# Another order of projection pairs, and two gate pairs moved into the attention, in a hybrid SSD and attention layer

## The chip, the cores and the metric

The kernel runs on one core of a Trainium2 chip. The metric is the device time of one execution in microseconds (us). The engines are TensorE (PE, its weight loads PEld), VectorE (DVE), ScalarE (ACT), GpSimd (POOL) and SyncE (SP), which issues most DMAs. Each engine works through its own instructions in order and waits on semaphores for the others.

## The reference

One layer over a sequence of 1024 positions with 1024 channels, all in float32, weights drawn at random. Cut to what matters:

```python
h = rmsnorm(x, pre_g)
z_ssm, xbc, dt_raw, q, k, v, f_raw, z_att, g_ssm, g_att = split(h @ w_in)
xbc = silu(causal_dwconv(xbc, conv_w, conv_b))         # 4 taps
xs, b, c = split(xbc)                                  # 16 heads of 64; 4 groups, state 128
y = ssd_chunked(xs, softplus(dt_raw + dt_bias), -exp(a_log), b, c, d_skip)   # chunks of 128
y_ssm = group_rmsnorm(y * silu(z_ssm)) * ssm_norm_g
log_f = log_sigmoid(f_raw + fgate_b)                   # per head
o = softmax(q k^T / 8 + F[t] - F[s], causal) @ v       # F = cumsum(log_f), 16 heads of 64
y_att = o * silu(z_att)
merged = sigmoid(g_ssm) * (y_ssm @ w_branch_ssm) + sigmoid(g_att) * (y_att @ w_branch_att)
out = x + rmsnorm(merged @ w_out, post_g)
```

## The kernel before

**Projections as a stream of pairs.** The large products (h times w_in, the two branch products and the last one) are cut into units of 128 output columns. Two units of one kind make a `Pair`, for instance ("z", 0) and ("z", 1). A pair is computed by a seven-product scheme of the Strassen kind over the two halves of the inner dimension, the two units and the two halves of the sequence. Each product is a step of 12 matmuls: four slices of the inner dimension, three matmuls each, since every operand is split into a rounded high part and a low rest (`h` and `l`; tiles `x0h`, `x0l` and so on for the moving side, `wop` for the weights). A step runs in two halves of 6 matmuls; a pair is 14 halves. Weights are prepared by sums (DVE, line 357 and others) and splits (ACT line 351, DVE line 352). Results are evicted by `keep` (ACT line 404) and `give` (lines 412 to 418), and a handler then does what the kind of pair needs: `conv` (b, c, x), `silu_gate` (z, za), `tanh_gate` (gs, ga), `parts` (q, k: high and low parts stored) or `values` (v: transposed on TensorE, later, by `turn_values()`). All but the convolution's results go to DRAM and come back when they are used.

**The order.** `order` lists the pairs of four groups, `late` the gates za (four), gs (three more) and ga (four), `ends` the branch products (wbs, wba) and the last product (merged). `Stream` runs them all in one sequence, and other work is put beside them by counting halves: `stream.halves(n)`, `stream.beside(generator)`, `stream.until(pair)`. A pair's first step is run before its predecessor's last two. Pairs before the index `double` have a PSUM bank of their own ("d") for one product; the later ones share bank "c" and run their steps in another order. Before the change `order` begins gs, q, b/c, x, z, k, v for group 0 and goes on with z, b/c, q, x, k, v for groups 1 to 3.

**The recurrence.** For each group the program runs the stream to the end of the group's x pair and 4 halves more, then `ssd(g)` beside the stream: 40 halves for eight chunks of 128, with loads of chunk sums (`csb`), decays on ACT, products on TensorE and POOL. At every chunk `turn_values()` takes at most one pending set of four transposes (tile `tr_v`). From the fifth chunk on z is loaded back for the gate. `gate_and_norm(g)` follows beside the stream with 22 halves; its last stores (ys_dram, line 1007) are on SP's queue. The 128x512 tiles `th` of the handlers come from a pool of four buffers.

**The attention.** Eight head pairs of six steps each. A step computes scores for two blocks of queries (`s`), adds F and takes a minimum (DVE line 1459), exponentiates (ACT line 1463, `ex`), transposes on TensorE (`pt`, line 133), evicts (`p`, lines 1481 and 1483) and, in the next step, multiplies with the values (`av`). Projection halves are put in twice per step by `fill(m, part)`: part 0 between the scores and the transposes, part 1 behind the transposes. How many is worked out from `weights` (a share for each head pair) and `rooms` (a share for each of the six steps and two parts), rounded to whole halves:

```python
share = weights[min(m // 6, NK - 1)] * rooms[m % 6][part]
to = stream.steps.index((ends[4], 6))
stream.halves(round((2 * (to - stream.at) - (stream.run is not None)) * share / left[0]))
```

Before the first scores q, k, F (tile `fb`) and v of the first head pair are loaded, and 14 halves of the stream run. While the last ga pair runs, the moving operands in SBUF are replaced one by one by those of the SSM branch (`ops_s`): loads, then splits on ACT (lines 277 and 280) and DVE (278 and 281). While the last wbs pair runs they are replaced by the attention branch's (`ops_a`), some of which come straight from the last head pair. Behind the attention the rest of the branch products and the last product follow.

The framework's planner places the engines' instructions in order by priority, with TensorE's order kept as written.

## Time and profile before

| | |
|---|---|
| runs | 1337.20, 1339.51, 1344.38 us; median 1339.51 |
| profiled execution | span 1338.1 us from the first to the last instruction; no other time of its own is listed |
| granted TensorE clock | 0.988 on average |
| busy | PE 95%, PEld 74%, DVE 76%, ACT 59%, POOL 23% |
| DMA | 233.59 MB, 175 GB/s on average |

Busy shares are shares of the span. Rows called windows give the busy time of each engine in a stretch, with the number of instructions in brackets, then the granted TensorE clock (1.00 is full), the DMA engines' share and GB/s. A row of waits names the waiting engine, tile and line, then what released it, the time in us, the number of times and the longest. Times in a timeline count from the span's start.

### The profile page before, as it was taken

Reading aid. Unit: us, or ns where it says so; the run is one execution under the profiler, and the core shown is the slowest. Engines: PE = TensorE matmul, PEld = TensorE weight load, DVE = VectorE, ACT = ScalarE, POOL = GpSimd, SP = SyncE. Lnnn points to the kernel's source line nnn. Section 1 sums busy time; section 2 is a strip of 40 time slices with the busy share of each in tenths; the row PEclk is TensorE's granted clock in tenths of the full one; section 3 lists DMA queues with packets and bytes.
Section 4 is the critical chain, followed back from the end, with each engine's and each line's share of the span. In section 5 each row is a group of like instructions: output and inputs, shape, how many; then the busy total and the mean of one; then the engine's idle time right before and its main releaser. Section 6 shows DMA issues by size and latency. Waiting matters only on the chain. (4 is left out here: it accounts for less than half of the span.)

```text
span 1338.1 us, 21044 instructions
## 1 busy us (share of the span) xinstructions
PE 1273.1 (95%) x7054; PEld 992.6 (74%) x7054; DVE 1016.8 (76%) x1977; ACT 787.4 (59%) x1726; POOL 303.6 (23%) x311
## 2 busy tenths in 40 slices
PE   6899999999999999999999999998879998889997
PEld 4678878777888888788877777776657666668886
DVE  7979986887888888888676667666876657676976
ACT  7645765466665666566556665666754545543664
POOL 3000440013300431034002132221121213235152
PEclk9999999999999999999999999999999999889999
DMA  7232543554446533654474566567855657545933
GB/s 287 70 116 66 164 136 121 155 171 157 127 126 202 166 120 121 198 170 130 135 267 151 180 201 204 183 228 241 277 194 185 189 190 244 182 149 183 368 127 102
DMA packets 154668, 233.59 MB, mean 175 GB/s; under 512 B 17216, under 2 KB 62656, under 8 KB 154560
## 3 DMA queue, kind: packets, MB, share of 16 engines
q1 hardware_dynamic: 142016, 205.53, 48.2%
q0 software_dynamic: 6400, 16.10, 3.2%
q10 hardware_dynamic: 6144, 10.62, 2.1%
q8 instruction: 55, 0.90, 0.3%
q14 instruction: 53, 0.43, 0.1%
HBM read 162.99 MB, written 72.34 MB: 176 GB/s over the span
## 5 line engine op out<-in xcount | busy, mean ns | idle before, releaser
L1463 ACT ACTIVATE ex<-ex,nm 128x512 f32<-128x512 f32 (+1 forms) x192 | 116.0, 605 | 154.2 <-DVE nm L1459 152.3
L352 DVE TENSOR_TENSOR wop<-sum,wop 128x512 fp32r<-128x512 f32 x180 | 138.3, 769 | 54.5 <-ACT wop L351 53.4
L351 ACT ACTIVATE wop<-sum 128x512 fp32r<-128x512 f32 x180 | 112.4, 625 | 78.1 <-DVE sum L357 29.6
L352 DVE TENSOR_TENSOR wop<-raw,wop 128x512 fp32r<-128x512 f32 x144 | 110.5, 768 | 43.6 <-ACT wop L351 42.6
L404 ACT ACTIVATE s<-pb 128x512 f32<-128x512 f32 x144 | 84.9, 589 | 90.2 <-PE pb L130 87.8
L130 PE MATMUL pc<-x3h,wop 128*128 128x512 f32 x384 | 133.1, 404 | 2.8 <-DVE th L414 1.7
L130 PE MATMUL pc<-x2h,wop 128*128 128x512 f32 x384 | 130.9, 399 | 2.3 <-DVE th L416 2.0
L130 PE MATMUL pb<-x4h,wop 128*128 128x512 f32 x384 | 130.3, 396 | 2.8 <-ACT x4h L277 2.1
L130 PE MATMUL pb<-x0h,wop 128*128 128x512 f32 x384 | 132.3, 401 | 0.0
L130 PE MATMUL pb<-x5h,wop 128*128 128x512 f32 x384 | 130.7, 399 | 1.0 <-ACT s L404 1.0
L130 PE MATMUL pb<-x6h,wop 128*128 128x512 f32 x384 | 129.0, 394 | 0.0
L1459 DVE CUSTOM_DVE_ANT_0 ex<-s,fb 128x512 f32<-128x512 f32 (+1 forms) x192 | 95.7, 550 | 36.8 <-PE s L130 36.8
L133 PE MATMUL pt<-ident,ex 128*128 128x128 f32 x576 | 81.3, 283 | 20.5 <-ACT ex L1463 19.8
L351 ACT ACTIVATE wop<-raw 128x512 fp32r<-128x512 f32 x144 | 89.5, 622 | 12.4 <-PE pc L130 6.1
L130 PE MATMUL pd<-x1h,wop 128*128 128x512 f32 x288 | 96.6, 394 | 0.0
L133 PEld LDWEIGHTS pt<-ident,ex 128*128 128x128 f32 x576 | 67.7, 143 | 35.9 <-ACT ex L1463 29.9
L130 PEld LDWEIGHTS pc<-x3h,wop 128*128 128x128 f32 x384 | 73.7, 192 | 22.0 <-issue 2.6
L130 PEld LDWEIGHTS pc<-x2h,wop 128*128 128x128 f32 x384 | 72.1, 188 | 20.8 <-DVE th L416 3.1
L130 PEld LDWEIGHTS pb<-x5h,wop 128*128 128x128 f32 x384 | 73.3, 191 | 18.5 <-ACT s L404 1.7
L130 PEld LDWEIGHTS pb<-x4h,wop 128*128 128x128 f32 x384 | 72.1, 188 | 19.7 <-ACT x4h L277 2.5
L130 PEld LDWEIGHTS pb<-x0h,wop 128*128 128x128 f32 x384 | 73.5, 191 | 16.3 <-issue 0.9
L130 PEld LDWEIGHTS pb<-x6h,wop 128*128 128x128 f32 x384 | 72.1, 188 | 16.1 <-issue 0.4
(310 smaller groups left out, 2965.8 us busy)
## 6 DMA issues: line engine op xcount, KB each, us to landing
raw<-in_wu SPq DMA_DIRECT2D x128, 256.0 KB, 4.1
csb<-cs_dram SPq DMA_DIRECT2D x32, 256.0 KB, 5.2
fb<-f_dram SPq DMA_DIRECT2D x16, 512.0 KB, 6.2
rb<-st_dram SPq DMA_DIRECT2D x48, 128.0 KB, 3.1
wd<-in_wo SPq DMA_DIRECT2D x40, 128.0 KB, 3.1
xt<-in_x SPq DMA_DIRECT2D x8, 512.0 KB, 5.9
gs_dram<-th ACTq DMA_DIRECT2D x16, 256.0 KB, 3.7
qh_dram<-th SPq DMA_DIRECT2D x16, 256.0 KB, 2.0
```

The costliest lines, as they stand in the source:

```text
L130: return tc.keep_in_program_order(nc.tensor.matmul(*args, **kw))
L133: return tc.keep_in_program_order(nc.tensor.transpose(out_, in_, idn))
L351: nc.scalar.activation(op[:, 0], src, AF.Copy)
L352: nc.vector.tensor_tensor(op[:, 1], src, op[:, 0], ALU.subtract)
L404: nc.scalar.activation(s, ps, AF.Copy)
L1459: nc.vector.tensor_tensor_reduce(o, s[e][:, 0:w], fb[hp, h][:, e, 0:w], 1.0, 3.0e38, ALU.add, ALU.min, nm)
L1463: pin(nc.scalar.activation(o, o, AF.Exp, scale=-1.0, bias=nm, accum_out=hd.at(hd.sm, i, h, e)))
```

## The change

In the groups the b/c pair comes first, then q, x, z, v, k. Group 0 begins with gs, q, b/c and goes on with x, z, v, k, so that only its k and v change places; in groups 1 to 3 z moves from the first place to behind x, and v ahead of k. The recurrence's index of the x pair goes from 3 to 2. The stream no longer runs to the end of the third za pair ahead of the attention but to the end of the first; `double` goes from three to one pair behind the groups. The weights of the attention's fill change.

```diff
     def groups_pairs(g):
         return [
-            both("z", g, lambda i: silu_gate(zg_dram, i)),
             Pair((("b", g), ("c", g)), (conv(g, "bt", 8 + g), conv(g, "ct", 12 + g))),
             both("q", g, lambda i: parts(qh_dram, ql_dram, i, -0.125)),
             Pair((("x", 2 * g), ("x", 2 * g + 1)), tuple(conv(g, f"xs{j}", 2 * g + j) for j in range(2))),
+            both("z", g, lambda i: silu_gate(zg_dram, i)),
+            both("v", g, values),
             both("k", g, lambda i: parts(kh_dram, kl_dram, i, 1.0)),
-            both("v", g, values),
         ]
...
-    order[0:4] = [both("gs", 0, lambda i: tanh_gate(gs_dram, i))] + [order[n] for n in (2, 1, 3, 0)]
+    order[0:2] = [both("gs", 0, lambda i: tanh_gate(gs_dram, i)), order[1], order[0]]
...
-        stream = Stream(order + late + ends, len(order) + 3, len(order) + len(late) + 4)
+        stream = Stream(order + late + ends, len(order) + 1, len(order) + len(late) + 4)
...
-            stream.until(by_group[g][3])
+            stream.until(by_group[g][2])
...
-    stream.until(late[2])
+    stream.until(late[0])
...
-        weights = (1.1, 1.1, 1.1, 1.1, 0.75, 0.95, 1.05, 0.85)
+        weights = (1.0, 1.0, 1.0, 1.0, 0.95, 1.05, 1.1, 0.95)
```

## The prediction

> **What bounds the kernel now.** I read the page first: busy times, then the slices, where TensorE and its granted clock thin out.

> ```profile
> span 1338.1 us, 21044 instructions
> PE 1273.1 (95%) x7054; PEld 992.6 (74%) x7054; DVE 1016.8 (76%) x1977; ACT 787.4 (59%) x1726; POOL 303.6 (23%) x311
> PE   6899999999999999999999999998879998889997
> PEclk9999999999999999999999999999999999889999
> ```

> TensorE is busy 95% of the span and its work is the same after the change. So the question is only where it waits. The 9s stop between slices 27 and 36, in the later part of the attention. For that I cut the span into stages: rows 1 to 4 below are the four groups, from one x pair's end to the next (the fourth ends with the last gated norm), row 5 the run-in to the attention, rows 6 to 13 the eight head pairs 0 to 7 (from the first softmax instruction of one to that of the next), row 14 the end.

> ```profile
> core 0: us, PE busy (x) PEld busy (x) DVE busy (x) ACT busy (x) POOL busy (x), PEclk, DMA share, GB/s
> 126.70:284.70 158.00, 154.38 (x783) 124.43 (x782) 130.66 (x212) 91.93 (x184) 34.41 (x30) 1.00 0.47 145
> 284.70:421.50 136.80, 136.19 (x715) 110.62 (x714) 114.00 (x192) 86.03 (x172) 30.94 (x29) 1.00 0.49 156
> 421.50:557.50 136.00, 135.64 (x707) 109.77 (x707) 114.99 (x192) 84.43 (x171) 30.59 (x28) 1.00 0.49 153
> 557.50:673.80 116.30, 115.94 (x624) 94.20 (x623) 95.20 (x155) 71.85 (x149) 25.43 (x25) 1.00 0.45 142
> 673.80:697.60 23.80, 21.78 (x107) 16.87 (x106) 16.57 (x31) 9.77 (x18) 0.64 (x2) 1.00 0.87 299
> 697.60:754.90 57.30, 57.30 (x392) 43.87 (x391) 36.93 (x102) 35.19 (x89) 8.98 (x12) 1.00 0.52 165
> 754.90:812.40 57.50, 57.37 (x392) 43.65 (x392) 36.81 (x100) 35.56 (x91) 15.11 (x19) 1.00 0.61 198
> 812.40:870.80 58.40, 58.08 (x394) 43.90 (x393) 39.80 (x103) 34.86 (x90) 13.85 (x19) 1.00 0.58 197
> 870.80:932.70 61.90, 59.85 (x402) 45.22 (x400) 42.54 (x107) 38.73 (x97) 14.20 (x19) 1.00 0.67 222
> 932.70:996.90 64.20, 54.18 (x355) 38.23 (x355) 47.20 (x118) 42.57 (x105) 9.22 (x14) 0.97 0.70 242
> 996.90:1053.30 56.40, 51.42 (x349) 36.95 (x349) 37.66 (x104) 28.55 (x79) 11.61 (x19) 0.97 0.57 186
> 1053.30:1115.40 62.10, 58.62 (x391) 43.58 (x388) 40.05 (x107) 33.28 (x87) 14.53 (x21) 0.97 0.66 209
> 1115.40:1184.30 68.90, 55.68 (x337) 38.55 (x335) 49.26 (x117) 40.77 (x104) 19.83 (x25) 0.91 0.61 190
> 1184.30:1338.10 153.80, 146.94 (x636) 120.91 (x636) 111.14 (x159) 75.85 (x151) 60.84 (x43) 0.98 0.56 191
> ```

> TensorE's idle time (length less busy) is 0.0, 0.1 and 0.3 us in head pairs 0 to 2, 2.0 in head pair 3, then 10.0, 5.0, 3.5 and 13.2, 31.7 us in the last four, at a granted clock of 0.97, 0.97, 0.97 and 0.91 against 1.00. No engine is full there. Their waits by name:

> ```profile
> PE pt L133 <- ACT ex L1463: 19.8, 28, 2.8
> PE av L130 <- ACT p L1483: 4.8, 5, 1.7
> PE av L130 <- DVE p L1481: 2.5, 1, 2.5
> PE pb L130 <- ACT x4h L277: 2.1, 1, 2.1
> ```

> 19.8 us are transposes waiting for the exponentials of the same step. What covers that stretch is the projection work put between a step's scores and its transposes. In head pairs 0 to 2 it is enough; in the last four it is not.

> **The unit.** In the chain, projection steps that wait for nothing read:

> ```profile
> 1192.34 2.72 PE pd L130 x12
> ```

> Twelve matmuls, one of a pair's seven products, take 2.72 us, so a half (six matmuls) takes 1.36 us and a pair of 14 halves 19.0 us.

> **The change, counted in halves.** Per group the recurrence with its norm spans 4 + 40 + 22 = 66 halves behind x. The distance from x to the next x is 84 halves for groups 1 to 3 in both orders, but for group 0 it is 98 before (z, k, v, then the next z, b/c, q, x) and 84 after (z, v, k, b/c, q, x). Behind the last x stand 66 halves and a filling-up to the end of the third za pair (4 more) before; after, the 66 halves already pass the end of the first za pair, so nothing is filled up. The attention thus begins at half 376 instead of 394, 18 halves earlier: 18 x 1.36 = 24.5 us leave a part of the program where TensorE idles 0.4 us in 116 (row 4). The same 18 halves come back inside the attention: 174 instead of 156 are shared out, and by the weights and rounding of fill() the head pairs get 22, 22, 22, 22, then 16, 17, 20, 15 before and 21, 22, 22, 21 after. Seventeen of the 18 land between scores and transposes, where the 19.8 us lie.

> **Term 1, out of the projection phase:** -24.5 us.

> **Term 2, into the attention:** +24.5 us of matmuls less what falls into waits. The pace without waits is head pair 0's: 57.3 us with 22 halves (29.9 us), so 27.4 us for attention itself; its 392 matmuls are 132 of projection and 260 others. By the same count the last four hold (355-260)/6 = 16, 15, 22 and about 16 halves in their windows (the slots' edges differ a little from the windows'), for which the pace gives 49.2, 47.8, 57.3 and 49.2 us; they took 15.0, 8.6, 4.8 and 19.7 more, 48 us together, of which idle is 31.7 and the rest slowed or late-issued matmuls. That is more than 24.5, so the upper bound is that all of it is absorbed: 24.5. The lower bound is 0: waits set by ScalarE and VectorE, which grow with the added work. For that speaks the change of operands to the SSM branch's, whose splits fall into head pair 4 (L280 on ScalarE, then L281 on VectorE, head pair 4's rows):

> ```profile
> 932.70:996.90 64.20, 9.24 (x16) 0.97 0.70 242
> 932.70:996.90 64.20, 11.24 (x16) 0.97 0.70 242
> ```

> This burst does not vanish. It hangs on the last ga pair (halves 490 to 504), which moves from the end of head pair 3 to the end of head pair 4, and it then runs beside slots of 3 halves instead of 2. In between, by the row of waits: 28 waits of transposes make 19.8 us; a step waits for up to four exponentials, so these are seven or eight steps with some 2.6 us each, and an added half takes its 1.36 us off each, 10 us; of the 7.3 us of av waits behind them I count a third, so step by step 12 us are absorbed. Since ScalarE and VectorE also catch up while TensorE has work, the rest shrinks too. I take 18, the middle between 12 and 24.5, because rows 6 to 8 show almost no wait at the very slot sizes that the last four will have: +6.5 us.

> The granted clock bears on this. Its loss over the last four rows is 64.2 x 0.03 + 56.4 x 0.03 + 62.1 x 0.03 + 68.9 x 0.09 = 11.7 us, and I let it shrink with the waits. [...]

> **Term 3, values before k.** turn_values() is called only inside the recurrence. In group 0 v ran third behind x, too late for its last two turns:

> ```profile
> L133 PE MATMUL tr_v<-ident,th x8: 272/272/328, 184.5 to 200.3; 128*128 128x128 f32 x8
> L133 PE MATMUL tr_v<-ident,th x24: 272/273/273, 303.4 to 345.0; 128*128 128x128 f32 x24
> L133 PE MATMUL tr_v<-ident,th x16: 272/273/273, 455.7 to 480.3; 128*128 128x128 f32 x16
> ```

> Group 0 (first row) does 8 of its 16 turns, group 1 makes them up from 303 us on. From 200 to 303 us two of the four 128x512 "th" buffers are held. In that stretch their users wait, TensorE at last:

> ```profile
> ACT th L651 <- DMA ql_dram<-th: 3.4, 2, 2.7
> ACT th L412 <- DMA qh_dram<-th: 2.6, 1, 2.6
> PE pc L130 <- DVE th L416: 2.0, 1, 2.0
> PE pc L130 <- DVE th L418: 0.8, 1, 0.8
> PE pc L130 <- DVE u L416: 0.3, 1, 0.3
> ```

> Row 1 of the stages idles 3.6 us where rows 2 to 4 idle 0.4 to 0.6. With v second behind x in every group all four turns fit: -3 us (ends 0 and -3.6).

> **z and k swapped beside the recurrence: 0.** Each gives four evictions, four ScalarE passes and four VectorE passes. z issues 4 stores on SP where k issues 8, both behind VectorE or ScalarE in SP's order, with the chunk sums' and weights' loads queued behind them. Group 0 already has z there, and its recurrence runs without more idle time than the bound of row 1, 3.6 us, from the other reason. z reaches memory by half 14 and is read at half 28 or later. Ends -1 and +2.

> **Start of the attention: +1.** The loads of q, k and F queue on SP behind the last norm's stores, and 14 halves (19.0 us) cover them. Before, 4 filling-up halves stood in between too:

> ```profile
> 674.31 0.45 SPq L1319 DMA_DIRECT2D q<-qh_dram  x1
> 677.80 0.47 SPq L1328 DMA_DIRECT2D fb<-f_dram  x1
> fb<-f_dram SPq DMA_DIRECT2D x2, 512.0 KB, 8.9
> 697.62 0.68 DVE L1459 CUSTOM_DVE_ANT_0 ex<-s,fb 128x512 f32<-128x512 f32 x1
> ```

> From the first load to the first F's landing: 677.8 + 8.9 - 674.3 = 12.4 us; used at 23.3 us. Less 4 halves (5.4 us) leaves 17.9, still 5 us to spare. What is late next would be F, then the scores' softmax. Two further pairs (za1, za2) now run in the form that shares one PSUM bank, at small waits: row 5 idles 2.0 us. Ends 0 and +4.

> **Sum:** -24.5 + 6.5 - 3 + 1 = -20.0 us against the profiled span of 1338.1, so 1318.1. The median of the runs is 1339.51, 1.4 above that span; on that footing 1319.5.

> **Rivals.**

> *The waits are not for lack of projection work.* ScalarE's and VectorE's bursts set the pace, and the added matmuls lengthen the head pairs by nearly all of their time: absorbed 0 to 8 us, sum -24.5 + 24.5 - (0 to 8) - 3 + 1 = -2 to -10, 1329 to 1337. For it: head pair 4 has VectorE 47.2 us busy against 36.9 in head pair 0. Against it: head pair 5 has no burst, only 37.7 us of VectorE and 28.6 of ScalarE, and still 5.0 us idle, with fewer halves as the one difference.

> *Slower: the last head pair becomes bound by VectorE.* The second change of operands (to the attention branch's) now starts with head pair 7 instead of late in 6. VectorE has 49.3 us there; 6 more halves at 16.57/14 = 1.2 us bring 7, together 56 us, as much as TensorE's 27.4 + 21 x 1.36 = 56. If the last output then comes late, everything behind it does. That head pair's splits now (L281 and L278):

> ```profile
> 1115.40:1184.30 68.90, 9.28 (x13) 0.91 0.61 190
> 1115.40:1184.30 68.90, 6.42 (x8) 0.91 0.61 190
> ```
> It decides if that and the following operand's wait (2.1 us now) grow by more than 20 us: the burst put wholly on the path, 13 + 8 splits of 0.7 us on VectorE behind 0.6 on ScalarE (by the rows of head pair 4), gives 21 x 1.3 = 27 us, so 1347. Against it: most of these splits are of rows finished heads earlier.

> *More than forecast.* All 24.5 absorbed and the slower clock gone: -28 to -32, 1307 to 1311.

> **Chances.** A change under 0.5% (6.7 us) cannot be told from none here. Forecast (1311 to 1329, its own range) 0.67; little absorbed 0.19, of which two thirds lie within 0.5% (above 1332.8); slower 0.06, one third of it beyond 0.5%; more than forecast 0.06; 0.02 for an order on ScalarE and VectorE that comes out worse all over. Faster 0.67 + 0.06 + 0.06 = 0.79, same 0.17, slower 0.04. The range is 1309 to 1336: it leaves out the best two microseconds of the bounds, the slower rival and the worst edge.

> **What would show it.** The first softmax instruction starts about 27 us earlier, near 670; the first group's idle falls below 1 us and its 16 turns lie in its own recurrence; head pairs 4 to 6 take 57 to 64 us each with 21 or 22 halves, and TensorE idle in the last four falls from 31.7 to about 15; the waits of transposes for exponentials halve. The splits of the first operand change start about 20 us later than head pair 4 does. Wrong, if the distance from the first softmax instruction to the end of head pair 7 grows by over 18 us from its 486.7, or if head pair 7 passes 78 us.

## The result and the profile after

The changed kernel takes 1329.76 us (median of 6 runs, 1326.76 to 1332.75) against 1337.07 us for the kernel before (6 runs beside it). The ratio is 0.9939, with 95% between 0.992 and 0.9958: faster by 0.6%, or 7.3 us, where 20 had been forecast. The profiled execution has a span of 1327.8 us, 10.3 less than the span before, and a time of 1329.54. The account below is made between the two spans; that they differ by 3 us more than the medians do is within what single executions of one kernel differ by.

From the page of the changed kernel: its span, its busy times, and TensorE and its granted clock in 40 slices.

```profile
span 1327.8 us, 21035 instructions
PE 1271.5 (96%) x7054; PEld 995.1 (75%) x7054; DVE 1021.1 (77%) x1977; ACT 789.8 (59%) x1726; POOL 304.2 (23%) x311
PE   6899999999999999899999999999989998899997
PEclk9899999999999999899999999999999999999999
```

The 9s now go on to slice 29, two slices further than before. But slice 17, which was full before, has an 8 in both rows. Cut into the same stages (group 0; the last group and its norm; the run-in to the attention; head pairs 0 and 4 to 7; the end):

```profile
core 0: us, PE busy (x) PEld busy (x) DVE busy (x) ACT busy (x) POOL busy (x), PEclk, DMA share, GB/s
128.30:265.30 137.00, 135.42 (x708) 109.89 (x707) 115.77 (x192) 85.08 (x170) 31.46 (x29) 1.00 0.48 151
...
538.00:656.40 118.40, 114.15 (x600) 91.59 (x599) 91.72 (x154) 72.14 (x149) 26.59 (x27) 0.97 0.45 140
656.40:679.80 23.40, 23.40 (x116) 18.86 (x115) 16.64 (x31) 9.93 (x18) 1.42 (x2) 1.00 0.90 318
679.80:740.80 61.00, 59.78 (x398) 44.81 (x397) 41.78 (x106) 35.50 (x90) 10.69 (x13) 1.00 0.48 158
...
916.70:977.70 61.00, 59.22 (x397) 44.44 (x396) 43.24 (x109) 38.94 (x98) 10.75 (x15) 1.00 0.73 244
977.70:1043.30 65.60, 59.20 (x379) 43.75 (x379) 50.40 (x123) 42.66 (x105) 9.54 (x17) 0.95 0.63 212
1043.30:1102.40 59.10, 57.54 (x389) 42.87 (x388) 41.08 (x108) 32.01 (x84) 13.45 (x21) 1.00 0.58 196
1102.40:1176.10 73.70, 64.12 (x385) 46.53 (x383) 53.87 (x124) 46.15 (x113) 20.11 (x26) 0.93 0.63 208
1176.10:1327.80 151.70, 144.75 (x636) 119.16 (x636) 115.74 (x163) 75.90 (x151) 64.90 (x45) 0.99 0.59 200
```

The second row is the loss. The kernel before needs 110.8 us for the same 66 halves, counted from the end of the last x pair:

```profile
557.50:668.30 110.80, 110.44 (x599) 89.67 (x598) 89.77 (x147) 68.11 (x142) 25.43 (x25) 1.00 0.45 141
```

| stretch | before, us | after, us | difference | forecast |
|---|---|---|---|---|
| start to end of group 0's x | 126.7 | 128.3 | +1.6 | 0 |
| group 0, to the next x | 158.0 (98 halves) | 137.0 (84 halves) | -21.0, of which 19.0 are the 14 halves | -19.0 - 3 |
| groups 1 and 2 | 272.8 | 272.7 | -0.1 | 0 |
| last group, 66 halves | 110.8 | 118.4 | +7.6 | 0 |
| run-in to the first softmax | 29.3 (18 halves) | 23.4 (14 halves) | -5.9, of which 5.4 are the halves | -5.4 + 1 |
| **first softmax starts** | 697.6 | 679.8 | -17.8 | -26.5 |
| head pairs 0 to 3 | 235.1 | 236.9 | +1.8 | 0 |
| head pairs 4 to 7 | 251.6 | 259.4 | +7.8 | +6.5 |
| behind the attention | 153.8 | 151.7 | -2.1 | 0 |
| **sum** | 1338.1 | 1327.8 | -10.3 | -20.0 |

The last four head pairs took the added halves nearly as forecast. Most of what is missing, 7.6 of 9.7 us, was lost before the attention, beside the last recurrence.

**What happens in the last group.** TensorE's waits in that stretch, after the change:

```profile
PE tr L133 <- DVE xs L778: 3.3, 1, 3.3
PE pc L130 <- ACT wop L351: 0.8, 1, 0.8
```

One wait of 3.3 us, for the last instruction of x's SiLU. The timeline of the changed kernel around it (start, duration, what; in brackets the idle time of the engine before it and what ended it):

```profile
545.24 0.33 SPq L247 DMA_DIRECT2D b_low<-wl  x1
...
545.66 1.73 SPq L344 DMA_DIRECT2D raw<-in_wv  x2
...
550.34 0.69 DVE L357 TENSOR_TENSOR sum<-raw 128x512 f32<-128x512 f32 x1 [1.26 <-DMA raw<-in_wv]
...
552.04 0.84 POOL L213 TENSOR_TENSOR wd<-wd 128x256 f32<-128x256 f32 x1 [13.66 <-DMA wd<-in_wo]
...
552.21 1.82 DVE L778 SCALAR_TENSOR_TENSOR xs<-th,xs 128x512 f32<-128x512 f32 x2
...
553.48 0.47 PE L133 MATMUL tr<-ident,xs 128*128 128x128 f32 x1 [3.29 <-DVE xs L778]
```

and SP's own waits from 535 to 552 us:

```profile
SPq L247 <- DVE wl L240: 9.6, 1, 9.6
```

Read upwards. TensorE waits for VectorE (L778). VectorE has stood 1.26 us at a weight sum (L357), ahead of L778 in its order, for v's weights to land. Those 1.26 us are only a part of the 3.3: for the rest VectorE has work of its own ahead of L778 and is behind. The loads were issued at 545.66 because SP had stood for 9.6 us at a store (L247) of something else: the *chores*. `weights_work()` prepares differences of the weights for the later products, one small item per half beside the recurrences, in a cycle of 39 halves: loads (L208) and stores (L195, L247) on SP, subtractions on POOL (L213), splits on ScalarE and VectorE (L240). Items of this list follow each other by count, not by what the recurrence is doing. With the last x pair 14 halves earlier, another place of the cycle meets the start of the last recurrence. This follows from the count of halves; no run separates that place from the new order of the pairs.

The clock nearly doubles the price. Windows of the changed kernel around the wait (the columns are those of the stages):

```profile
549.16:552.57 3.41, 1.04 (x6) 0.56 (x4) 2.23 (x4) 1.72 (x4) 0.53 (x1) 1.00 0.82 239
552.57:559.40 6.83, 5.92 (x16) 4.84 (x17) 6.83 (x13) 4.30 (x11) 0.93 (x2) 0.50 0.29 70
```

From 552.57 us on, near the end of the wait, the granted clock is half for 6.83 us. Idle time in the last group is 4.3 us against 0.4, and the same work is busy 3.7 us longer: together the 7.6.

The second part is not fixed. Some of the runs below change only what lies behind this stretch, so beside the last recurrence they are written like the changed kernel (the order alone but for about its last ten halves):

| run | 66 halves, us | TensorE idle, us | at half clock, us |
|---|---|---|---|
| the order alone | 115.3 | 4.5 | 0 |
| subtractions on VectorE | 115.9 | 4.6 | 0 |
| 12 halves ahead of the first scores | 116.0 | 4.7 | 0 |
| 16 halves | 116.8 | 4.1 | 3.4 |
| the old weights | 118.2 | 5.2 | 3.4 |
| the change | 118.4 | 4.3 | 6.8 |
| 18 halves | 119.2 | 5.1 | 6.8 |

All of them idle 4.1 to 5.2 us there, against 0.4 before. How much of the 3.7 us of slower clock comes on top differs from one profiled execution to the next, with 0, 3.4 or 6.8 us at half clock; the part on the clock below has what the traces show of it.

### The profile page after: what moved, and what is told of

Read it like the earlier page. It is cut to its first block, busy times and chain, and to the rows that moved or that the text cites. A ratio compares the mean times of both kernels' runs of the same rounds, so it can differ in the third digit from the quotient of the medians.

```text
span 1327.8 us, 21035 instructions
## 1 busy us (share of the span) xinstructions
PE 1271.5 (96%) x7054; PEld 995.1 (75%) x7054; DVE 1021.1 (77%) x1977; ACT 789.8 (59%) x1726; POOL 304.2 (23%) x311
## 4 chain that ended last, share of the span: by engine, by line
PE 64%; DVE 11%; DMA 10%; ACT 8%; issue 5%; SPq 1%; POOL 0%; DVEq 0%; ACTq 0%
PE pb L130 26%; PE pc L130 14%; PE pd L130 5%; PE av L130 4%; PE s L130 4%; PE pt L133 4%; ACT ex L1463 2%; PE yps L130 2%; DMA raw<-in_wu 2%; DVE wop L352 2%; ACT wop L351 1%; DVE sum L357 1%; PE tr L133 1%; PE st L130 1%; DVE ex L1459 1%
## 5 line engine op out<-in xcount | busy, mean ns | idle before, releaser
L1463 ACT ACTIVATE ex<-ex,nm 128x512 f32<-128x512 f32 (+1 forms) x192 | 116.1, 607 | 146.7 <-DVE nm L1459 142.7
L352 DVE TENSOR_TENSOR wop<-sum,wop 128x512 fp32r<-128x512 f32 x178 | 141.4, 795 | 66.0 <-ACT wop L351 65.4
L351 ACT ACTIVATE wop<-sum 128x512 fp32r<-128x512 f32 x178 | 111.4, 626 | 77.7 <-DVE sum L357 25.6
L352 DVE TENSOR_TENSOR wop<-raw,wop 128x512 fp32r<-128x512 f32 x146 | 107.0, 734 | 42.7 <-ACT wop L351 41.6
L130 PE MATMUL pc<-x3h,wop 128*128 128x512 f32 x384 | 131.8, 401 | 1.9 <-DVE th L418 0.9
L130 PE MATMUL pb<-x0h,wop 128*128 128x512 f32 x384 | 133.0, 404 | 0.0
L130 PE MATMUL pb<-x6h,wop 128*128 128x512 f32 x384 | 131.2, 399 | 1.2 <-ACT s L404 1.2
L130 PE MATMUL pb<-x4h,wop 128*128 128x512 f32 x384 | 130.2, 396 | 0.7 <-ACT x4h L1178 0.7
L130 PE MATMUL pc<-x2h,wop 128*128 128x512 f32 x384 | 130.4, 398 | 0.3 <-DVE u L756 0.3
L130 PE MATMUL pb<-x5h,wop 128*128 128x512 f32 x384 | 129.1, 395 | 0.7 <-ACT s L404 0.7
L1459 DVE CUSTOM_DVE_ANT_0 ex<-s,fb 128x512 f32<-128x512 f32 (+1 forms) x192 | 95.7, 552 | 33.1 <-PE s L130 33.1
L133 PE MATMUL pt<-ident,ex 128*128 128x128 f32 x576 | 80.5, 285 | 11.6 <-ACT ex L1463 10.6
L130 PE MATMUL pd<-x1h,wop 128*128 128x512 f32 x272 | 91.2, 394 | 0.0
L130 PEld LDWEIGHTS pc<-x3h,wop 128*128 128x128 f32 x384 | 73.3, 191 | 20.5 <-ACT wop L351 1.9
L133 PEld LDWEIGHTS pt<-ident,ex 128*128 128x128 f32 x576 | 68.9, 145 | 24.8 <-ACT ex L1463 19.2
L130 PEld LDWEIGHTS pb<-x6h,wop 128*128 128x128 f32 x384 | 73.0, 190 | 18.3 <-ACT s L404 1.6
L130 PEld LDWEIGHTS pb<-x0h,wop 128*128 128x128 f32 x384 | 74.3, 193 | 16.5 <-issue 0.7
L130 PEld LDWEIGHTS pb<-x4h,wop 128*128 128x128 f32 x384 | 72.3, 188 | 17.5 <-ACT x4h L1178 1.2
L213 POOL TENSOR_TENSOR wd<-wd 128x256 f32<-128x256 f32 x32 | 32.7, 1021 | 229.7 <-DMA wd<-in_wo 128.9
L130 PEld LDWEIGHTS pb<-x5h,wop 128*128 128x128 f32 x384 | 72.1, 188 | 17.4 <-ACT s L404 1.1
## 6 DMA issues: line engine op xcount, KB each, us to landing
fb<-f_dram SPq DMA_DIRECT2D x16, 512.0 KB, 6.7
xt<-in_x SPq DMA_DIRECT2D x8, 512.0 KB, 5.9
```

The costliest lines, as they stand in the source:

```text
L130: return tc.keep_in_program_order(nc.tensor.matmul(*args, **kw))
L133: return tc.keep_in_program_order(nc.tensor.transpose(out_, in_, idn))
L213: pin(nc.gpsimd.tensor_tensor(t[out_], t[a_], t[b_], ALU.subtract))
L351: nc.scalar.activation(op[:, 0], src, AF.Copy)
L352: nc.vector.tensor_tensor(op[:, 1], src, op[:, 0], ALU.subtract)
L1459: nc.vector.tensor_tensor_reduce(o, s[e][:, 0:w], fb[hp, h][:, e, 0:w], 1.0, 3.0e38, ALU.add, ALU.min, nm)
```

## The experiments

Each ran beside the kernel before; ratios are to that, with their 95% interval. Edits are against the changed kernel if nothing else is said.

**The order alone**, with the two za pairs and the weights left as they were:

```diff
-        stream = Stream(order + late + ends, len(order) + 1, len(order) + len(late) + 4)
+        stream = Stream(order + late + ends, len(order) + 3, len(order) + len(late) + 4)
...
-    stream.until(late[0])
+    stream.until(late[2])
...
-        weights = (1.0, 1.0, 1.0, 1.0, 0.95, 1.05, 1.1, 0.95)
+        weights = (1.1, 1.1, 1.1, 1.1, 0.75, 0.95, 1.05, 0.85)
```

> The changed order of pairs alone: the attention begins at half 394 as before, with the old weights, so no projection work is moved into it. Theory A (the 7.6 us that the last group's recurrence lost, 118.4 us against 110.8 for the same 66 halves, belong to the order, in which x's convolution comes out late on VectorE): that loss is there too, the first group's gain of 2 us as well, together 3 to 6 us slower than before (1340 to 1343). Theory B (the loss belongs to the earlier start of the attention or is chance): 2 to 3 us faster than before (1334 to 1335).

Measured 1339.84 us, ratio 1.0017 (0.9999 to 1.0036). The last group's 66 halves:

```profile
536.10:651.40 115.30, 110.81 (x600) 89.61 (x599) 89.98 (x151) 71.42 (x149) 28.09 (x27) 1.00 0.47 145
```

4.5 us are lost there without moving any projection work into the attention, 3.5 of them in one wait for x, and the clock stays at 1.00. The idle part of the loss thus belongs to the new order, not to the move into the attention. The order by itself gains nothing, but it is not slower by the 3 to 6 us expected either.

**v ahead of k in group 0 alone**, against the kernel before:

```diff
-    order[0:4] = [both("gs", 0, lambda i: tanh_gate(gs_dram, i))] + [order[n] for n in (2, 1, 3, 0)]
+    order[0:6] = [both("gs", 0, lambda i: tanh_gate(gs_dram, i))] + [order[n] for n in (2, 1, 3, 0, 5, 4)]
```

> The kernel before with one edit: in group 0 v comes ahead of k, so that all its turns fit into its own recurrence. Theory A (two of four th buffers held from 200 to 303 us cause the waits of the first group): its idle time of 3.6 us falls under 1.5 us and the kernel gains 2 to 3.5 us (1333.5 to 1335). Theory B (these waits come from VectorE's load beside the second group's convolution, whatever the buffers): the turns move, the idle time stays, no gain.

Measured 1332.28 us, ratio 0.9943 (0.9925 to 0.9961). Group 0, the last group, and the turns of group 0's values:

```profile
127.10:280.90 153.80, 153.80 (x791) 125.75 (x790) 128.62 (x212) 92.93 (x186) 32.61 (x30) 1.00 0.48 153
552.20:662.50 110.30, 110.30 (x600) 89.73 (x599) 88.81 (x146) 67.59 (x141) 25.06 (x25) 1.00 0.46 143
L133 PE MATMUL tr_v<-ident,th x16: 272/272/273, 161.0 to 185.6; 128*128 128x128 f32 x16
```

Sixteen turns lie in their own recurrence, idle time in group 0 goes from 3.6 us to nothing, and its 98 halves take 4.2 us less. The last group stays whole. The first softmax begins 7.6 us earlier. This exchange of two pairs is by its interval worth as much as the whole change, and more than its expected 2 to 3.5 us. What exceeds the 4.2 us lies in small parts (groups 1 and 2 1.5 us, last group 0.5, run-in 1.8), for which the run shows no single cause.

**Two halves more ahead of the last recurrence.**

```diff
-            stream.halves(4)
+            stream.halves(6 if g == NG - 1 else 4)
```

> The changed kernel with 6 instead of 4 halves of projection between the last group's x pair and its recurrence (2.7 us more for the convolution). Theory A (the single wait of 3.3 us of the transposes for x on VectorE, with the slower clock behind it, is the last group's loss): the wait goes, that stage is 4 to 7 us nearer to 110.8 us, and the kernel gains 3 to 6 us on the changed one (1324 to 1327). Theory B (VectorE is behind as a whole there): the wait turns up a few halves later and the time stays within 2 us of 1329.8.

Measured 1323.1 us, ratio 0.9877 (0.9849 to 0.9905). TensorE's waits there:

```profile
PE yps L130 <- DVE m L849: 1.7, 1, 1.7
PE tr L133 <- DVE xs L778: 0.9, 1, 0.9
```

The wait for x shrinks to 0.9 us; less the two halves' 2.7 us the stretch takes 116.7 us, 1.7 better. The rest of the gain lies in the attention, which I had not expected.

**The old weights of the fill** in the changed kernel (the last pair of lines of the first diff alone).

> The changed kernel with the old weights of the fill: the same 174 halves in the attention, but 24 in each of the first four head pairs and 16 to 20 in the last four. Theory A (the waits of the last four head pairs are for lack of projection work between scores and transposes): most of the 18.8 us that the added halves took up there come back as idle time, 1336 to 1341. Theory B (the waits follow ScalarE's and VectorE's bursts): within 3 us of 1329.8.

Measured 1336.7 us, ratio 0.9982 (0.9961 to 1.0004). Its last four head pairs take 57.5, 67.5, 67.1 and 72.5 us, TensorE idle 24.3 us of it against 19.3, and its transposes wait more:

```profile
PE pt L133 <- ACT ex L1463: 10.5, 16, 3.0
```

So it matters where the 174 halves go: with more of them in the last four head pairs the kernel gains some 6 us (0.9982 against 0.9939). With eight halves fewer the last four take 5.2 us longer than in the changed kernel; their idle time rises by 5 us, not by most of the 18.8 expected. That the waits there are for lack of projection work, as Term 2 has it, rests on this run.

**All chores one half later**, to see whether the 3.3 us are a matter of phase:

```diff
-                stream.chores += list(weights_work())
+                stream.chores += [None] + list(weights_work())
```

> The changed kernel with the chores that prepare the last product's weights begun one half later; no work is added or taken away. It moves GpSimd's subtractions of 128x256 against VectorE's instructions beside the recurrences. Theory A (the last group's wait of 3.4 us, and with it the 3.4 us of half clock, hangs on where such instructions fall together): that wait changes by 1 us or more in either direction, the time by 2 to 7 us. Theory B (it is settled by the order of pairs alone): within 1.5 us of the changed kernel's 1329.8, the same wait at the same place.

Measured 1328.96 us, ratio 0.9911 (0.9896 to 0.9927); the last group takes 118.5 us. Its waits:

```profile
PE st L130 <- POOL xe L871: 4.5, 1, 4.5
PE tr L133 <- DVE xs L778: 0.9, 1, 0.9
```

The wait for x shrinks to 0.9 us, and one of 4.5 us for POOL is there instead. Moving the phase moved the place; the loss stayed, and the median is within 1 us of the changed kernel's.

**The stores of L247 two halves later**, so that SP meets them when they are ready (two more empty items before each store, as many fewer behind).

```diff
                 yield go
+                yield None
+                yield None
                 yield lambda: pin(self.queue.dma_start(self.lows[name][j][:, cols], state["low"]))
```

> The changed kernel with the chores' stores of low parts (line 247, on SP's queue) issued two halves later, the pauses behind them shortened as much. In the changed kernel such a store stands 9.6 us on SP at 535.6 to 545.2 us for VectorE, with the loads of v's weights queued behind it; their sum on VectorE waits 1.3 us for the landing, x's last SiLU behind that sum in VectorE's order, TensorE 3.3 us for x, and then the clock is halved for 6.8 us. Theory A (that queue is the last group's loss): the wait of the transposes for x falls under 1.5 us, the stage of 66 halves from 118.4 to 110 to 113 us, 4 to 8 us faster than the changed kernel. Theory B (VectorE alone is too full): the wait stays at 3 us or turns into another of the same length; within 2 us.

Measured 1335.52 us, ratio 0.9982 (0.9962 to 1.0003). The wait for x falls to 1.4 us, and again the POOL wait of 4.5 us appears:

```profile
PE st L130 <- POOL xe L874: 4.5, 1, 4.5
PE tr L133 <- DVE xs L781: 1.4, 1, 1.4
```

The last group takes 120.2 us, and group 1 is longer too. SP's stand is how the loss comes about at this phase, not why the last group loses.

**The chores behind the last recurrence** (the time means nothing here: their whole work then stands alone on the path, 1460.29 us).

```diff
-            if g == 0:
-                stream.chores += list(weights_work())
...
         stream.beside(norm)
+        stream.chores += list(weights_work())
         stream.do_chores()
```

> The changed kernel with all chores issued at once behind the last recurrence instead of beside the recurrences. The time as a whole says nothing, since the attention's loads then stand behind them; what is read is the stretch of 66 halves from the last x pair to the end of the last norm. Theory A (chores on SP, GpSimd, ScalarE and VectorE are the last group's loss): 108 to 111 us and no wait over 1 us for x, xe or m there. Theory B (the order of pairs alone fills VectorE there): 116 us or more, with the wait for x.

```profile
532.80:643.40 110.60, 110.60 (x600) 89.67 (x599) 87.24 (x145) 67.40 (x140) 21.57 (x20) 1.00 0.40 126
```

In the new order, without chores, TensorE does not stand for a moment in the last group: 110.6 us, as before the change. So the waits of the last group, and with them its half clock, come from the chores in this order of pairs. The chores alone do not do it: the kernel before has them too and takes 110.8 us.

**A shorter cycle of the chores**, 37 halves instead of 39:

```diff
-                yield from (None,) * 4
+                yield from (None,) * 2
```

> The changed kernel with a pause of 2 instead of 4 halves between the chores' parts, so that other chores (a cycle of 37 instead of 39 halves) fall beside the beginning of each recurrence: fewer of them beside the last one (one subtraction and one low part instead of the same with their stores and a fetch bunched). Theory A (the chores beside the beginning of the last recurrence are its loss): the 66 halves change by 2 us or more from 118.4, in that direction the time. Theory B (the last group is slow without them as well): 118 within 1.5 us.

Measured 1326.63 us, ratio 0.9923 (0.9903 to 0.9943); profiled span 1320.8.

```profile
537.90:649.30 111.40, 111.07 (x599) 89.52 (x598) 91.92 (x150) 69.15 (x145) 26.73 (x25) 1.00 0.48 144
```

With all chores done, but in another phase, the last group takes 111.4 us, and the first softmax starts at 673.2, 6.6 us earlier than in the changed kernel. The shorter cycle also ends the chores 16 halves sooner, in the last group, so this run is not one of phase alone; but the wait at the start of that recurrence, where chores still run, falls from 3.3 to 0.4 us. By the medians the gain is smaller, 3 us with overlapping intervals; the profiled execution is the fastest of its six.

**A priority for x's convolution and SiLU** in the planner's order (the last multiplications of both under `tc.high_priority()`).

> The changed kernel with the convolution and the last SiLU step of the x units placed ahead of other work by the planner on ScalarE and VectorE; the same instructions. Theory A (x comes out of VectorE late only because weight splits and sums stand ahead of it): the last group's wait of 3.4 us and its half clock go, the stage of 66 halves falls from 118.4 to 110 to 113 us, the kernel gains 4 to 8 us on the changed one (1322 to 1326). Theory B (VectorE is full there): the wait comes back at the weights' splits, no gain, or up to 5 us slower since three other groups now have their splits later.

Measured 1330.85 us, ratio 0.9939 (0.9921 to 0.9956); the wait is still 3.6 us, since the weight sum that waits for v's load stayed ahead on VectorE. The edit did not do what it was for, so the run says little.

**How much stands between the last norm and the first scores.** Four runs changed the 14 halves there, one of them together with the later stores.

```diff
-        for _ in range(14):
+        for _ in range(16):
```

> The changed kernel with 16 instead of 14 halves of projection between the recurrence's end and the first scores: the attention as in the run with two more halves ahead of the last recurrence (it begins at half 392, 172 halves are shared out), the projection phase as in the changed kernel. Theory A (most of that run's 8 us came from where the pairs' steps fall against the attention's steps, since its last group was only 1.7 us better): 4 to 7 us faster than the changed kernel, 1323 to 1326. Theory B (they came from the last group's recurrence): within 2 us of 1329.8.

> The changed kernel with 18 halves ahead of the first scores (the attention begins at half 394, 170 halves are shared out). Theory A (14 halves were too few to cover the loads ahead of the attention, since the weights' loads queue behind those of q, k, F and v and VectorE's sums stand ahead of the first softmax instruction; from 16 on they are enough): head pair 0 takes 57 to 59 us as with 16, the time is within 3 us of 1320 or up to 4 us above it, for 2 halves fewer in the last head pairs. Theory B (16 is a lucky place of steps against each other): 1326 or more.

> The changed kernel with 12 halves ahead of the first scores (176 shared out). Theory A (too little cover for the loads): the first softmax instruction comes 4 to 6 us behind the first scores instead of 3.6, head pair 0 takes 62 to 65 us, 2 to 4 us slower than the changed kernel, 1331 to 1335. Theory B (places of steps against each other): no such order; 1320 to 1330 is possible.

> The run with 16 halves ahead of the first scores and the later stores together. If the two losses are separate, the gains add: 4 to 8 us under 1320, at 1312 to 1316. If the later store brings nothing by itself, 1320 within 2 us.

| halves | us | ratio (95%) | first softmax to the end of head pair 7, us |
|---|---|---|---|
| 12 | 1326.93 | 0.9914 (0.9892 to 0.9936) | 498.8 |
| 14 (the change) | 1329.76 | 0.9939 (0.992 to 0.9958) | 496.3 |
| 16 | 1319.97 | 0.9855 (0.9838 to 0.9872) | 489.8 |
| 18 | 1321.65 | 0.9861 (0.9835 to 0.9888) | 485.2 |
| 16, later stores | 1330.64 | 0.9936 (0.9915 to 0.9956) | |

Head pair 0 took 57.3 us before and 61.0 after the change. With 16 halves (rows of head pairs 0 and 7), and with 12 (head pair 0):

```profile
677.00:734.60 57.60, 57.47 (x392) 43.78 (x392) 40.50 (x105) 34.84 (x89) 10.86 (x13) 1.00 0.51 160
...
1100.40:1166.70 66.30, 57.52 (x376) 41.66 (x374) 49.94 (x120) 45.05 (x111) 20.91 (x26) 1.00 0.67 228
```

```profile
673.30:731.30 58.00, 56.73 (x386) 42.73 (x385) 41.49 (x108) 35.76 (x91) 10.40 (x13) 1.00 0.50 168
```

Too little cover for the first loads is not the cause: 12 halves cover less, and head pair 0 takes 58.0 us. Sixteen halves have the lowest median of all, 17 to 22 us under the kernel before by its interval, though the interval of 18 overlaps. From 14 to 16 the attention loses two halves, 2.7 us, but gets 6.5 shorter. Of the other 3.8 us the clock accounts for most: in the attention the profiled execution with 14 halves is at half clock for 20.5 us, the one with 16 for 13.7, and half of the difference, an estimate from the granted 0.50, is 3.4 us. The timed executions agree: the median of their mean clocks is 0.988 with 14 halves and 0.991 with 16. Why there are fewer such stretches is open: the pairs' steps then fall on other steps of the attention, and no run separates that. The 16 halves with the later stores fit neither forecast; their last group takes 121.9 us.

**The shorter cycle and 16 halves together.**

> The short pause together with 16 halves ahead of the first scores, as the candidate for the fastest. If the pause gains 3 us or more by itself, 1314 to 1317; if not, 1320 within 3 us.

Measured 1322.21 us, ratio 0.9891 (0.9872 to 0.991), with a last group of 111.6 us and the shortest profiled span of all, 1314.8. By the timed runs it is not better than the 16 halves alone (1319.97), so the two gains do not add.

**Sixteen subtractions of the first change of operands on VectorE instead of POOL**, to see whether VectorE's stretched instructions (below) hold up head pairs 0 and 1:

```diff
-                    pin(nc.gpsimd.tensor_tensor(t[out_], t[a_], t[b_], ALU.subtract))
+                    pin((nc.vector if third is None else nc.gpsimd).tensor_tensor(t[out_], t[a_], t[b_], ALU.subtract))
```

> The changed kernel with the 16 subtractions of 128x512 for the SSM branch's operands (line 213, in head pairs 0 to 3) on VectorE instead of GpSimd. In the traces each VectorE instruction that took over 0.25 us more than the others of its kind overlaps a GpSimd one; at 738 us of the changed kernel one takes 2.23 us instead of 0.69 beside a subtraction of 1.30 us on GpSimd, and the transposes of that step wait 3.6 us. Theory A (this overlap makes the waits of head pairs 0 and 1): their 3.5 us of idle time fall to under 1 us, 2 to 4 us faster than the changed kernel, though VectorE has 16 x 0.69 = 11 us more. Theory B (VectorE's own load makes them): no gain or up to 4 us slower.

Measured 1324.09 us, ratio 0.9893 (0.9875 to 0.9911). The waits of head pairs 0 and 1, first in this run, then in the changed kernel:

```profile
PE pt L133 <- ACT ex L1463: 4.0, 9, 1.3
```

```profile
PE pt L133 <- ACT ex L1463: 3.4, 6, 1.9
```

The waits did not go, so that theory falls. The better median is not explained by its trace: the profiled execution (span 1329.3 us, time 1331.05) is the slowest of its six, the others took 1323.2 to 1325.3 us. It stays open.

## Why the prediction was right in kind and wrong in size

**Term 1, -24.5, and "z and k swapped: 0": the steps that failed.** The halves left the projection phase as counted (14 from group 0, 4 from the filling-up). But Term 1 took for granted that the last group keeps its 0.4 us of idle time, and the swap was costed by the evictions, passes and stores of z and k. What was not costed is the work that goes by count beside the recurrence. The prediction named the weights' loads that queue on SP, but not the chores' stores that stand in front of them. In place of 0 stood +7.6 us in the profiled execution, outside the ends of -1 and +2: about 4 us of idle time (4.1 to 5.2 us in the seven kernels of the table, 0.4 before) and 3.7 of half clock, which not every execution has. Shown by the order alone (115.3 us), by the chores taken away (110.6) and by another cycle (111.4). That it is the phase of the cycle is argued from the count.

**Term 3, -3: right in kind.** The turns are where they were forecast to be:

```profile
L133 PE MATMUL tr_v<-ident,th x16: 272/272/273, 162.2 to 186.9; 128*128 128x128 f32 x16
```

In the changed kernel it brings 2.0 us and 1.6 us of idle time stay (forecast: below 1); in the old order 4.2 us, above the upper end of 3.6. The end was set by idle time alone, while busy time fell too (154.38 to 153.80 us).

**Start of the attention, +1: measured -0.5** up to the first softmax. The scores no longer come at once into a free VectorE, though:

```profile
675.35 0.69 DVE L357 TENSOR_TENSOR sum<-raw 128x512 f32<-128x512 f32 x1 [1.78 <-DMA raw<-in_wu]
675.49 0.97 PE L130 MATMUL s<-k,q 64*128 64x512 f32 x6
...
679.76 0.68 DVE L1459 CUSTOM_DVE_ANT_0 ex<-s,fb 128x512 f32<-128x512 f32 x1
```

The first softmax starts 2.5 us behind the end of the first step's scores (0.3 before): a weight sum waits for its load, issued behind those of q, k, F and v, and it and six more instructions stand ahead on VectorE. "What is late next" was not F but the weights.

**Term 2, +6.5: right.** The last four head pairs take 7.8 us more for 24.5 us of matmuls, and 2.1 come back behind them (before the change a half-clock stretch that begins in head pair 7 reaches 5 us into the end): +5.7, so 18.8 are absorbed where 18 were taken. That it came so close is in part luck, since 18 was the middle of two bounds. One reading in it is off: by its own count head pair 7 held (337-260)/6 = 13 halves before, not about 16, so it took 24 us over the pace and not 19.7, and the four 52 and not 48; this only strengthens its upper bound. Their waits, to be held against the 19.8 us in 28 waits of before:

```profile
PE av L130 <- ACT p L1483: 8.8, 4, 4.6
PE pt L133 <- ACT ex L1463: 7.2, 11, 1.8
PE av L130 <- DVE p L1481: 1.0, 1, 1.0
PE pb L130 <- ACT s L404: 0.7, 1, 0.7
```

The transposes' waits more than halve. What is late next are the values' products: their waits go from 7.3 to 9.8 us. Idle time falls from 31.7 to 19.3 us (forecast: 15), the clock's loss from 11.7 to 65.6 x 0.05 + 73.7 x 0.07 = 8.4 us. Head pairs 4 and 6 lie in the forecast 57 to 64 us, 5 does not (65.6): the splits of the first change of operands begin 31.8 us behind the start of head pair 4 (forecast: about 20), and 14 of the 20 on ScalarE fall into head pair 5, where TensorE idles 6.4 us. The attention as a whole grows by 9.6 us, under the limit of 18, and head pair 7 stays below 78.

**Not forecast:** head pairs 0 to 3 at +1.8 us (head pair 0 +3.7, 1 and 2 together +1.1, 3 -3.0), and 1.6 us ahead of group 0, where nothing was changed and the runs lie anywhere between 126.0 and 128.9.

**The rivals.** "Not for lack of projection work" gave the right range of time for a wrong reason: the waits did give way. VectorE as the bound of head pair 7 did not come about, though that head pair lengthened from 68.9 to 73.7 us with VectorE busy 53.87 of them.

```profile
933.34:936.75 3.41, 1.55 (x8) 0.98 (x9) 1.67 (x9) 3.33 (x10) 0.00 (x0) 1.00 1.05 403
```

```profile
546.85:550.26 3.41, 1.67 (x8) 1.08 (x6) 1.86 (x4) 2.12 (x4) 0.44 (x1) 1.00 1.02 299
550.26:553.68 3.42, 1.64 (x9) 1.45 (x10) 3.42 (x5) 2.04 (x4) 0.57 (x1) 1.00 0.64 131
```

In the changed kernel the wait of 3.3 us lay for the most part in one window, in which TensorE was busy for 1.04 of 3.41 us. In the traces of the two kernels together, from some 60 us on to shortly before the end, each of the 8 full-clock windows of the grid with TensorE busy for less than 43% of it is followed by half clock, and none of the 696 with more than 64%. Of the 12 between these, 4 are followed by it (45, 48, 51 and 56% busy) and 8 are not (48 to 61%), so the busy share is not the whole rule; what else decides is open. The grid lies differently in the two executions (552.57 us of the one and 936.75 us of the other are 112.55 times 3.413 us apart), so that whether a given wait costs clock is in part chance is my estimate from this and from the table of the 66 halves.

## What to carry to other kernels

When the order of work changes, list everything that goes beside it by count, and ask for each what it will now stand next to; a queue worked through in order (here SP, 9.6 us at a store that waits for a split) passes a stall on to loads that have nothing to do with it. A wait on the chain can be a matter of phase: shifting the cause by a step only moved it here (3.3 us for x became 0.9, and 4.5 for POOL), so test by taking the whole periodic work away, as one run did here. And try the smallest part of a change alone: two pairs exchanged in group 0 were worth as much as the whole. Before a wait is priced by one profile, look whether half clock followed it there: beside the last recurrence the seven executions of the table have 0, 3.4 or 6.8 us of it.

## What the runs showed of the hardware

Some of VectorE's instructions were stretched beside POOL's. In the changed kernel 99 VectorE instructions take over 0.25 us more than the lower quartile of their form; every one overlaps a POOL instruction, and together they lose some 71 us (before the change: 98, with about the same loss). One of them, ahead of a wait of TensorE:

```profile
737.99 2.23 DVE L352 TENSOR_TENSOR wop<-raw,wop 128x512 fp32r<-128x512 f32 x1
738.37 1.30 POOL L213 TENSOR_TENSOR x<-x,th 128x512 f32<-128x512 f32 x1
...
742.34 0.33 PE L133 MATMUL pt<-ident,ex 128*128 128x128 f32 x1 [1.86 <-ACT ex L1463]
```

2.23 us for a form that takes 0.69 otherwise. Only instructions that read two tensors are among the 99 (80 TENSOR_TENSOR and 19 SCALAR_TENSOR_TENSOR, of 288 of these two operations that overlap a computing instruction of POOL); of 53 instructions of other operations that overlap one none is stretched. Why the one kind is and the other is not, the traces do not show.

The wait of 3.3 us of TensorE at 550 to 553 us of the changed kernel costs 7 us, since half clock follows it. With 12 halves ahead of the first scores TensorE idles 4.65 us in the 66 halves, against 4.25 in the changed kernel, and the clock stays full:

```profile
537.00:653.00 116.00, 111.35 (x599) 89.48 (x598) 91.30 (x154) 72.06 (x150) 28.13 (x27) 1.00 0.47 143
```

In these 66 halves TensorE is busy for 111.35 us in that run and for 114.15 in the changed kernel, where 6.83 us are at half clock: 2.8 us more, about half of the 5.92 us in which TensorE is busy in that stretch.
